# Loading x and the first weight chunk of a two-layer decoder trunk by quarters, with masks and norm vectors loaded later

## The chip, the cores and the metric

The kernel runs on one core of a Trainium2 chip. The metric is device time in microseconds (us) of one execution. Five engines work side by side, each through its own instructions in a fixed order: TensorE (PE in the profile, with its weight loads as PEld), VectorE (DVE), ScalarE (ACT), GpSimd (POOL) and SyncE (SP), which here only issues transfers. Transfers between the chip's main memory (HBM) and the on-chip memories are issued by SP, ACT or POOL and run on 16 DMA engines that all queues share.

## What is computed

The reference runs two post-norm layers on x (256 tokens of 1024 values). Every sub-layer is added to ALPHA times its input and normalized. Only the first feed-forward stage (layer 0, `ffn1`) and the start of the program are touched by the change:

```python
def _post_norm(x, y, g, b):
    z = (ALPHA * x + y).astype(jnp.float32)
    mu = z.mean(-1, keepdims=True)
    var = jnp.square(z - mu).mean(-1, keepdims=True)
    return ((z - mu) * lax.rsqrt(var + LN_EPS) * g + b).astype(x.dtype)

def _swiglu(x, w_in, w_out):
    gate, up = jnp.split(x @ w_in, 2, axis=-1)
    return (jax.nn.silu(gate) * up) @ w_out

for layer in range(DEPTH):
    x = _post_norm(x, FFN_RES_WEIGHT * _swiglu(x, *ffn1[layer]), *ln1[layer])
    mix = ...   # layer 0: short convolution and dilated attention; layer 1: mLSTM and stick-breaking attention
    x = _post_norm(x, mix, *ln2[layer])
    x = _post_norm(x, FFN_RES_WEIGHT * _swiglu(x, *ffn2[layer]), *ln3[layer])
```

## The kernel before

**Weights.** All weight matrices are cut into chunks of 1 MB, numbered in the order of use. Chunk 0 is the gate half of the first 256 columns of the first `w_in`, chunk 1 the up half of the same columns, chunk 2 the next gate half, and so on. The class `Weights` keeps three stages. A chunk is loaded into one of 3 `raw` buffers (`RAW`, line 27) by SP; it is then split in 4 units of a quarter each (`unit`, lines 72 to 91): ACT casts the quarter into a high part `hi` (line 86), and DVE subtracts it from the raw values to make the low part `lo` (line 87). Both lie in one of 5 `hl` buffers. A `raw` buffer can be loaded anew when the last quarter of its chunk has been split, and a later load stands behind an earlier one on SP's queue.

**Matmuls.** x is turned (transposed) on PE, 128 columns at a time, and split in the same way into `xx`, a high and a low part. For each chunk PE makes 16 wide matmuls (`wide`, line 235: `hi` times both parts of x, 128x512) and 16 cross matmuls (`cross`, line 239: `lo` times the high part of x, 128x256), into two PSUM banks out of a pool of four called `mm`. A bank is read out by ACT (line 425) and DVE (line 426, `join`), and only then can a later chunk's matmuls write to it.

**The start.** `start` (line 947) runs under `manual_schedule`: the instructions written in it keep their order among themselves on each engine. Everything else is placed by a scheduler, which may put an instruction of later work between them. PE first makes 9 idle matmuls on a zero tile, turns the first half of x (both token blocks), makes 3 more idle ones and turns the second half. Chunk 0 is then multiplied by quarters, two rows of 128 at a time (`mmB2`, line 252), so that it can begin when the first quarter of the weights and the first half of x are there.

**Transfers at the start.** x comes in four pieces of 256 KB (half a row for each of two token blocks), one block on SP, the other on ACT's queue. Chunks 0 and 1 come in quarters of 256 KB (`load_quarters`, line 48), chunk 2 and all later ones in one transfer. Then stand the masks (`msk`, lines 219 and 221: a pattern of 192 KB and a norm gain of 256 KB), used in the mixers much later, and the gain and bias of the first norm (`gb`, line 225, 512 KB each), used at the end of the stage.

**Scaling.** The residual ALPHA * x is made in place by ACT (line 483), two instructions of 128x1024.

Of the kernel before, what the change touches and what calls it, by code (L numbers as in the profile page):

```python
# [11 lines left out]
F32 = mybir.dt.float32  # L12
# [3 lines left out]
OP = mybir.AluOpType  # L16

P = 128
S = 256
# [3 lines left out]
ALPHA = math.sqrt(2.0)  # L23
# [7 lines left out]
class Weights:  # L31
# [16 lines left out]
    def load_quarters(self):  # L48

        i = self.loaded  # L50
        (ap,), k, c = self.chunks[i]
        self.raw[i] = self.raw_pool.tile([P, k * c], F32, tag="raw", name=f"raw{i}")
        rv = self.raw[i].rearrange("p (k c) -> p k c", k=k)
        for j in range(4):
            self.nc.sync.dma_start(rv[:, 2 * j:2 * j + 2, :], ap[:, 2 * j:2 * j + 2, :])
        self.loaded += 1

    def load(self, upto):
        while self.loaded < min(upto, len(self.chunks)):
# [74 lines left out]
def kernel(ctx: ExitStack, tc: tile.TileContext, a, cmask, out):  # L134
    nc = tc.nc
# [10 lines left out]
    def hp():  # L146
        return tc.high_priority(offset=HP)

    def nm(s):
        uid[0] += 1  # L150
        return f"{s}_{uid[0]}"
# [10 lines left out]
    def GR():  # L162
        return g_pool.tile([P, 1024], F32R, tag="g", name=nm("gr")).rearrange(
            "p (j h t) -> p j h t", j=2, h=2)

    def ACC():
        return ps_acc.tile([P, 512], F32, tag="acc", name=nm("acc"))

    def MM():
        return ps_mm.tile([P, 512], F32, tag="mm", name=nm("mm"))  # L170


    def cols(w, c0):
        return ([a[w][:, c0:c0 + 256].rearrange("(k p) c -> p k c", p=P)], 8, 256)
# [16 lines left out]
    first = cols("l1_mix_w_in", 3080)  # L191
# [5 lines left out]
    W = Weights(nc, raw_pool, w_pool, chunks)  # L197
# [4 lines left out]
    xx = const.tile([P, 8, 2, S], F32R, name="xx")  # L202
    xh, xl = xx[:, :, 0, :], xx[:, :, 1, :]
    X = [const.tile([P, D], F32, name=f"X{t}") for t in range(2)]
    for h in range(2):
        for t in range(2):
            hs = slice(h * 512, (h + 1) * 512)
            (nc.sync, nc.scalar)[t].dma_start(X[t][:, hs], a["x"][0, t * P:(t + 1) * P, hs])
    W.load_quarters()
    W.load_quarters()  # L210
    W.load(RAW)
    ident = const.tile([P, P], F32, name="ident")
    make_identity(nc, ident)
# [2 lines left out]
    Y = const.tile([P, D], F32, name="Y")  # L216
    gb = const.tile([P, 2, D], F32, name="gb")
    msk = const.tile([P, 896], F32, name="msk")
    nc.sync.dma_start(msk[:, 0:384], cmask)
    src = a["l1_mlstm_norm_g"]  # L220
    nc.sync.dma_start(msk[:, 384:896], bass.AP(tensor=src.tensor, offset=src.offset, ap=[[0, P], [1, 512]]))

    def bcast(dst, name, n, eng=None):
        src = a[name]
        (eng or nc.gpsimd).dma_start(dst, bass.AP(tensor=src.tensor, offset=src.offset, ap=[[0, P], [1, n]]))

    def load_gb(pre):
        bcast(gb[:, 0, :], pre + "_g", D, nc.sync)
        bcast(gb[:, 1, :], pre + "_b", D, nc.sync)
# [12 lines left out]
    def mmB1(i, banks, between=None):  # L242

        hi, lo = W.get(i)
        for f, w in ((wide, hi), (cross, lo)):
            if between and f is cross:
                between()
            for j in banks:
                for kt in range(8):
                    f(w, kt, j, banks[j])  # L250

    def mmB2(i, banks):
        hi, lo = W.views(i)
        for kt in range(0, 8, 2):
            for f, w in ((wide, hi), (cross, lo)):
                for j in range(2):
                    for k in (kt, kt + 1):
                        f(w, k, j, banks[j])

    def mmA1(i, t, bank, between=None):  # L260
        hi, _ = W.get(i)
# [37 lines left out]
    def split(hi, lo, src):  # L299
        nc.scalar.copy(hi, src)  # L300
        nc.vector.tensor_tensor(lo, src, hi.bitcast(F32), OP.subtract)  # L301


    def transpose_x(t, halves=(0, 1), scale=True):
        for hf in halves:
            b = MM()
            for j in range(4):
                c = hf * 512 + j * P
                nc.tensor.transpose(b[:, j * P:(j + 1) * P], X[t][:, c:c + P], ident)  # L309
            ks = slice(hf * 4, hf * 4 + 4)  # L310
            ts = slice(t * P, (t + 1) * P)
            with hp():
                split(xh[:, ks, ts], xl[:, ks, ts], b.rearrange("p (k t) -> p k t", k=4))
        if scale:
            nc.scalar.mul(X[t], X[t], ALPHA)
# [91 lines left out]
    def stagger(n, done, mm):  # L407

        ids = W.take(n)
        for t in range(2):  # L410
            for c in range(n):
                if t == 0 and c == n - 1:
                    transpose_x(1)
                b = MM()
                mm(ids[c], t, b)
                if t == 1:
                    W.free(ids[c])
                W.pump()
                done(t, c, b)
# [14 lines left out]
    def swiglu(gate, bank):  # L434

        u = joined(bank)
        nc.vector.scalar_tensor_tensor(u, gate, 0.5, u, OP.mult, OP.mult)  # L437
        return u

    def silu(bank):  # L440
        sg = joined(bank)
        nc.scalar.activation(sg, sg, AF.Silu)  # L442
        return sg

    def ffn(ln, staggered, nxt, last=False):
        ys = []
        todo = []

        def tr(t, gs):
            b = ACC()  # L450
            for p in range(2):
                for j in range(2):
                    nc.tensor.transpose(b[:, (2 * p + j) * P:(2 * p + j + 1) * P],
                                        gs[p][:, j * P:(j + 1) * P], ident)
            ts = slice(t * P, (t + 1) * P)
            for p in range(2):
                split(ys[p][:, :, 0, ts], ys[p][:, :, 1, ts],
                      b[:, p * 256:(p + 1) * 256].rearrange("p (j t) -> p j t", j=2))

        p0 = 0  # L460
        if staggered:
            p0 = 2
            ys = [GR(), GR()]
            gs = {0: [], 1: []}

            half = []

            def done(t, c, bank):
                if c % 2 == 0:
                    half.append(silu(bank))  # L470
                    return
                gs[t].append(swiglu(half.pop(), bank))
                if t == 1 and c == 1:
                    tr(0, gs[0])

            stagger(4, done, mmA1)
            todo.append(lambda: tr(1, gs[1]))
        for p in range(p0, NPAIR):
            if p == 4:
                load_gb(ln)  # L480
                if not staggered:
                    for t in range(2):
                        nc.scalar.mul(X[t], X[t], ALPHA)
            y = GR()
            ys.append(y)
            ig, iu = W.take(2)
            sg = []
            if p == 0:
                banks = [MM(), MM()]
                start(banks)  # L490
                W.pump()
            if p > 0:
                banks = {0: MM(), 1: MM()}
                mmB1(ig, banks)
            W.free(ig)
            for j in range(2):
                sg.append(silu(banks[j]))
                W.pump()
            while todo:
                todo.pop()()  # L500
            banks = {0: MM(), 1: MM()}
            mmB1(iu, banks)
            W.free(iu)
            W.pump()
            for j in range(2):
                g = swiglu(sg[j], banks[j])
                split(y[:, j, 0, :], y[:, j, 1, :], g)
                if j == 0:
                    W.pump()
        out_proj(ys, nxt, last)  # L510
# [436 lines left out]
    def start(banks):  # L947
        def idle(n):
            for _ in range(n):
                nc.tensor.matmul(wb, warm[:, 0:P], warm, start=True, stop=True)  # L950

        wb = MM()
        with tc.manual_schedule():
            idle(9)
            for t in range(2):
                transpose_x(t, (0,), False)
            idle(3)
            W.unit()
            for t in range(2):
                transpose_x(t, (1,), False)  # L960
                W.unit()
            W.unit()
            mmB2(0, banks)

    def f2_1():
        ffn("l1_ln3", True, None, last=True)
# [5 lines left out]
    def f1_1():  # L972
        ffn("l1_ln1", True, m1)

    def f2_0():
        ffn("l0_ln3", True, f1_1)
# [49 lines left out]
```

## Time and profile before

| | us |
|---|---|
| median of 3 runs | 988.82 |
| lowest and highest | 988.48, 989.24 |
| the profiled execution's own time | 989.54 |
| its span, first to last instruction | 987.8 |
| PE busy in the span | 976.6 |
| DVE, ACT, POOL busy | 703.6, 601.3, 24.0 |

A profile row gives a start and a duration in us from the span's first instruction; "idle before" names the idle time of the engine just ahead of the row and what ended it. A row with "x16" joins 16 instructions that follow each other without a gap. The time around the span is 989.54 - 987.8 = 1.74 us. PE is busy in all but some 11 us, so a microsecond counts where PE waits, and those waits lie at the start and at the end.

### The profile page before, as it was taken

To read this page: it belongs to the slowest core of one execution; us is meant where nothing else is said; L and a number is where in the kernel's file an instruction comes from. 1 tells how busy PE (TensorE), PEld (TensorE's weight loads), DVE (VectorE), ACT (ScalarE), POOL (GpSimd) and SP (SyncE) were. 2 spreads that over 40 slices of the span, in tenths; PEclk is the share of its full clock that TensorE was granted. 3 is DMA by queue.
4 is the path that set the end of the run, shared out by engine and by line. 5 is a ranking of instruction groups with operands and counts; after the bars stand their busy time and mean duration, and the time that the engine had idled before them with its cause. 6 is when DMAs were issued, how large, how long until landed. Compare 5 with 4: busy or idle time off the path is not lost.

```text
span 987.8 us, 14559 instructions
## 1 busy us (share of the span) xinstructions
PE 976.6 (99%) x5408; PEld 843.3 (85%) x5408; DVE 703.6 (71%) x1466; ACT 601.3 (61%) x1307; POOL 24.0 (2%) x62
## 2 busy tenths in 40 slices
PE   9999999999999999999999999999999999999997
PEld 7888888888878888888888888888888888888886
DVE  4987764678958877754687777547997788777534
ACT  6875654559847756553566665436887676565520
POOL 2000000010000000000000000001000100000000
PEclk9999999999999999999999999999999999999999
DMA  9875556474426756465475554646734267565611
GB/s 322 290 244 186 196 188 208 134 257 144 155 85 214 251 177 204 178 208 177 151 256 188 190 194 173 212 128 214 233 133 146 86 213 256 179 206 171 212 45 42
DMA packets 137495, 183.89 MB, mean 186 GB/s; under 512 B 4304, under 2 KB 121680, under 8 KB 137424
## 3 DMA queue, kind: packets, MB, share of 16 engines
q1 hardware_dynamic: 136720, 182.17, 55.4%
q8 instruction: 42, 0.69, 0.3%
q10 hardware_dynamic: 576, 0.79, 0.2%
q0 software_dynamic: 128, 0.01, 0.1%
q14 instruction: 29, 0.24, 0.1%
HBM read 181.90 MB, written 1.05 MB: 185 GB/s over the span
## 4 chain that ended last, share of the span: by engine, by line
PE 93%; DMA 2%; DVE 2%; ACT 2%; issue 0%; POOL 0%; DVEq 0%; POOLq 0%; ACTq 0%
PE mm L235 33%; PE mm L239 17%; PE acc L293 9%; PE acc L297 9%; PE acc L295 9%; PE mm L265 7%; PE mm L270 4%; DMA raw<-in_l_ffn_w_in_dram 2%; DVE hl L87 1%; PE acc L606 1%; PE mm L309 1%; PE mm L552 1%; ACT hl L86 1%; PE acc L546 0%; PE acc L547 0%; DMA X<-in_x_dram 0%
## 5 line engine op out<-in xcount | busy, mean ns | idle before, releaser
L87 DVE TENSOR_TENSOR hl<-raw,hl 128x512 fp32r<-128x512 f32 (+1 forms) x664 | 427.1, 687 | 89.1 <-ACT hl L86 82.7
L86 ACT CAST hl<-raw 128x512 fp32r<-128x512 f32 (+1 forms) x664 | 379.7, 621 | 108.8 <-PE acc L297 43.2
L235 PE MATMUL mm<-xx,hl 128*128 128x512 f32 x1472 | 357.4, 392 | 2.1 <-DVE t L426 1.1
L235 PEld LDWEIGHTS mm<-xx,hl 128*128 128x128 f32 x1472 | 269.0, 188 | 55.5 <-DVE t L426 1.7
L239 PEld LDWEIGHTS mm<-xx,hl 128*128 128x128 f32 x1472 | 189.8, 191 | 7.2
L239 PE MATMUL mm<-xx,hl 128*128 128x256 f32 x1472 | 195.4, 284 | 0.0
L425 ACT COPY t<-mm 128x256 f32<-128x256 f32 x182 | 66.7, 369 | 139.1 <-PE mm L239 127.3
L426 DVE TENSOR_TENSOR t<-mm,t 128x256 f32<-128x256 f32 x182 | 76.9, 424 | 97.2 <-ACT t L425 94.7
L293 PE MATMUL acc<-hl,gr 128*128 128x512 f32 (+1 forms) x416 | 128.7, 387 | 0.0
L295 PE MATMUL acc<-hl,gr 128*128 128x512 f32 (+1 forms) x416 | 127.5, 384 | 0.0
L297 PE MATMUL acc<-hl,gr 128*128 128x512 f32 (+1 forms) x416 | 127.1, 384 | 0.0
L297 PEld LDWEIGHTS acc<-hl,gr 128*128 128x128 f32 x416 | 77.1, 188 | 15.3 <-DVE gr L301 0.4
L295 PEld LDWEIGHTS acc<-hl,gr 128*128 128x128 f32 x416 | 77.2, 188 | 15.1
L293 PEld LDWEIGHTS acc<-hl,gr 128*128 128x128 f32 x416 | 76.0, 188 | 14.6 <-issue 0.6
L265 PE MATMUL mm<-hl,xx 128*128 128x512 f32 x336 | 85.1, 395 | 0.1
L265 PEld LDWEIGHTS mm<-hl,xx 128*128 128x128 f32 x336 | 60.5, 189 | 11.2 <-DVE t L426 0.3
L442 ACT ACTIVATE t<-t 128x256 f32<-128x256 f32 x88 | 36.7, 419 | 22.6 <-DVE t L426 22.5
L270 PEld LDWEIGHTS mm<-hl,xx 128*128 128x128 f32 x336 | 45.6, 190 | 3.1
L270 PE MATMUL mm<-hl,xx 128*128 128x256 f32 x336 | 47.1, 283 | 0.0
L328 ACT ACTIVATE t<-X,st 128x512 bf16<-128x512 f32 x22 | 15.7, 716 | 50.7 <-DVE st L324 50.7
L322 DVE SCALAR_TENSOR_TENSOR X<-acc,X 128x512 f32<-128x512 f32 x22 | 14.3, 690 | 42.3 <-PE acc L297 42.3
L437 DVE SCALAR_TENSOR_TENSOR t<-t,t 128x256 f32<-128x256 f32 x88 | 37.4, 425 | 2.6
(166 smaller groups left out, 565.3 us busy)
## 6 DMA issues: line engine op xcount, KB each, us to landing
raw<-in_l_ffn_w_in_dram SPq DMA_DIRECT2D x86, 1024.0 KB, 5.0
raw<-in_l_ffn_w_out_dram SPq DMA_DIRECT2D x44, 1024.0 KB, 4.9
raw<-in_l_mix_w_in_dram SPq DMA_DIRECT2D x26, 1024.0 KB, 5.2
raw<-in_l_mix_w_out_dram SPq DMA_DIRECT2D x8, 1024.0 KB, 4.9
gb<-in_l_ln_g_dram SPq DMA_DIRECT2D x6, 512.0 KB, 5.5
gb<-in_l_ln_b_dram SPq DMA_DIRECT2D x6, 512.0 KB, 5.1
raw<-in_l_ffn_w_in_dram SPq DMA_DIRECT2D x8, 256.0 KB, 7.3
X<-in_x_dram ACTq DMA_DIRECT2D x2, 256.0 KB, 4.3
```

The costliest lines, as they stand in the source:

```text
L86: self.nc.scalar.copy(hi[at], r[at])
L87: self.nc.vector.tensor_tensor(lo[at], r[at], hi[at].bitcast(F32), OP.subtract)
L235: nc.tensor.matmul(bank, hi[:, kt, j * P:(j + 1) * P], xx[:, kt].rearrange("p h t -> p (h t)"), start=kt == 0, stop=False)
L239: nc.tensor.matmul(bank[:, S:2 * S], lo[:, kt, j * P:(j + 1) * P], xh[:, kt, :], start=False, stop=kt == 7)
L265: nc.tensor.matmul(bank, xh[:, kt, ts], hl[:, kt].rearrange("p h c -> p (h c)"), start=kt == 0, stop=False)
L270: nc.tensor.matmul(bank[:, 256:512], xl[:, kt, ts], hi[:, kt, :], start=False, stop=kt == 7)
L293: nc.tensor.matmul(accs[c][:, 0:w], yh, hi[:, k, c:c + w], start=st, stop=False)
L295: nc.tensor.matmul(accs[c][:, 0:w], yh, lo[:, k, c:c + w], start=False, stop=False)
L297: nc.tensor.matmul(accs[c][:, 0:w], yl, hi[:, k, c:c + w], start=False, stop=sp)
L425: nc.scalar.copy(dst, bank[:, 256:512])
L426: nc.vector.tensor_tensor(dst, bank[:, 0:256], dst, OP.add)
L437: nc.vector.scalar_tensor_tensor(u, gate, 0.5, u, OP.mult, OP.mult)
```

## The change

It has four parts. (1) x comes in eight quarters of 128 KB (256 columns of a token block), and SP issues a quarter of x and a quarter of chunk 0 in turn; ACT issues the other block's four quarters. (2) `start` turns x by quarters into banks of the pool `acc`, splits each with `keep`, and puts the turning of the third and fourth quarter behind the matmuls of the first and second. (3) The masks, and the gain and bias of the first norm, are loaded at the fifth column pair (p == 4): GpSimd writes two values of `ys[3]` (the result of the fourth pair) into `msk` and `gb`, and the transfers that overwrite these must wait for that. (4) The two scalings of x move from ACT to GpSimd.

```diff
     def load_quarters(self):
         i = self.loaded
+        self.loaded += 1
         (ap,), k, c = self.chunks[i]
         self.raw[i] = self.raw_pool.tile([P, k * c], F32, tag="raw", name=f"raw{i}")
         rv = self.raw[i].rearrange("p (k c) -> p k c", k=k)
         for j in range(4):
             self.nc.sync.dma_start(rv[:, 2 * j:2 * j + 2, :], ap[:, 2 * j:2 * j + 2, :])
-        self.loaded += 1
+            yield
...
-    for h in range(2):
+    first = W.load_quarters()
+    for q in range(4):
+        qs = slice(q * 256, (q + 1) * 256)
         for t in range(2):
-            hs = slice(h * 512, (h + 1) * 512)
-            (nc.sync, nc.scalar)[t].dma_start(X[t][:, hs], a["x"][0, t * P:(t + 1) * P, hs])
-    W.load_quarters()
-    W.load_quarters()
+            (nc.sync, nc.scalar)[t].dma_start(X[t][:, qs], a["x"][0, t * P:(t + 1) * P, qs])
+        next(first)
+    for _ in W.load_quarters():
+        pass
     W.load(RAW)
...
-    nc.sync.dma_start(msk[:, 0:384], cmask)
-    src = a["l1_mlstm_norm_g"]
-    nc.sync.dma_start(msk[:, 384:896], bass.AP(tensor=src.tensor, offset=src.offset, ap=[[0, P], [1, 512]]))
+    def load_msk():
+        nc.sync.dma_start(msk[:, 0:384], cmask)
+        src = a["l1_mlstm_norm_g"]
+        nc.sync.dma_start(msk[:, 384:896], bass.AP(tensor=src.tensor, offset=src.offset, ap=[[0, P], [1, 512]]))
...
-    def mmB2(i, banks):
+    def mmB2(i, banks, kt):
         hi, lo = W.views(i)
-        for kt in range(0, 8, 2):
-            for f, w in ((wide, hi), (cross, lo)):
-                for j in range(2):
-                    for k in (kt, kt + 1):
-                        f(w, k, j, banks[j])
+        for f, w in ((wide, hi), (cross, lo)):
+            for j in range(2):
+                for k in (kt, kt + 1):
+                    f(w, k, j, banks[j])
...
             if p == 4:
+                if not staggered:
+                    late = ys[3].bitcast(F32)
+                    nc.gpsimd.tensor_copy(msk[:, 0:385:384], late[:, 0, 0, 0:2])
+                    nc.gpsimd.tensor_copy(gb[:, :, 0:1], late[:, :, 0, 0:1])
+                    load_msk()
+                    for t in range(2):
+                        nc.gpsimd.tensor_scalar(X[t], X[t], ALPHA, None, op0=OP.mult)
                 load_gb(ln)
-                if not staggered:
-                    for t in range(2):
-                        nc.scalar.mul(X[t], X[t], ALPHA)
...
+        def turned(q):
+            b = ACC()
+            for t in range(2):
+                for k in range(2):
+                    c = (2 * q + k) * P
+                    nc.tensor.transpose(b[:, k * S + t * P:k * S + (t + 1) * P], X[t][:, c:c + P], ident)
+            return b
+
+        def keep(q, b):
+            ks = slice(2 * q, 2 * q + 2)
+            split(xh[:, ks, :], xl[:, ks, :], b.rearrange("p (k t) -> p k t", k=2))
+
         wb = MM()
         with tc.manual_schedule():
             idle(9)
-            for t in range(2):
-                transpose_x(t, (0,), False)
+            b0 = turned(0)
+            W.unit()
+            keep(0, b0)
             idle(3)
+            b1 = turned(1)
+            keep(1, b1)
             W.unit()
-            for t in range(2):
-                transpose_x(t, (1,), False)
-                W.unit()
-            W.unit()
-            mmB2(0, banks)
+            for q in range(4):
+                mmB2(0, banks, 2 * q)
+                if q < 2:
+                    b = turned(q + 2)
+                    keep(q + 2, b)
+                    W.unit()
```

The diff does not tell where the scheduler puts the instructions, so the order in the two built programs is shown at three places.

The first place is ACT's queue from the first cast on. In the kernel before, `hl_144` and `raw_88` are chunk 0, `hl_202` and `raw_93` chunk 1, `hl_221` chunk 2, and `mm_127` to `mm_156` the banks with turned x. Before:

```order
L300 CAST xx<-mm_127 128x4x128
L300 CAST xx<-mm_134 128x4x128
L86 CAST hl_144<-raw_88 128x2x256
L300 CAST xx<-mm_147 128x4x128
L86 CAST hl_144<-raw_88 128x2x256
L300 CAST xx<-mm_156 128x4x128
L86 CAST hl_144<-raw_88 128x2x256 x2
L86 CAST hl_202<-raw_93 128x2x256 x4
L86 CAST hl_221<-raw_98 128x2x256 x3
L425 COPY t_207<-mm_113 128x256
```

After the change `hl_134` and `raw_86` are chunk 0, `hl_204` and `raw_97` chunk 1, `hl_223` and `raw_102` chunk 2, and `acc_129`, `acc_142`, `acc_159`, `acc_176` the four turned quarters of x:

```order
L87 CAST hl_134<-raw_86 128x2x256
L87 CAST hl_204<-raw_97 128x2x256 x2
L305 CAST xx<-acc_129 128x2x256
L87 CAST hl_204<-raw_97 128x2x256 x2
L305 CAST xx<-acc_142 128x2x256
L87 CAST hl_134<-raw_86 128x2x256
L305 CAST xx<-acc_159 128x2x256
L87 CAST hl_134<-raw_86 128x2x256
L87 CAST hl_223<-raw_102 128x2x256 x2
```

Casts of chunks 1 and 2 now stand between those of x and chunk 0: two quarters of chunk 1 ahead of the first quarter of x. On DVE the subtractions stand in the same order, one for each of these casts.

The second place follows on ACT's queue right behind the rows above; `hl_274` and `raw_185` are chunk 3, and `mm_115` is the first of chunk 0's two banks:

```order
L305 CAST xx<-acc_176 128x2x256
L87 CAST hl_134<-raw_86 128x2x256
L87 CAST hl_223<-raw_102 128x2x256 x2
L87 CAST hl_274<-raw_185 128x2x256 x2
L430 COPY t_209<-mm_115 128x256
L430 COPY t_219<-mm_116 128x256
```

The read of chunk 0's banks stands behind two casts of chunk 3 here; before, it stood behind three of chunk 2 (the last two rows of the first fence). On DVE one subtraction of chunk 3 stands ahead of its part of that read.

The third place is SP's queue. Before, the masks and the first norm's vectors stood between chunk 2 (`raw_98`) and chunk 3 (`raw_167`):

```order
L67 DMA raw_98<-in_l_ffn_w_in_dram 128x8x256
L219 DMA msk<-pattern_mask_dram 128x384
L221 DMA msk<-in_l_mlstm_norm_g_dram 128x512
L225 DMA gb<-in_l_ln_g_dram 128x1024
L225 DMA gb<-in_l_ln_b_dram 128x1024
L67 DMA raw_167<-in_l_ffn_w_in_dram 128x8x256
```

After the change they stand between chunk 14 (`raw_780`) and chunk 15 (`raw_829`), and SP waits there for GpSimd's two small copies:

```order
L68 DMA raw_780<-in_l_ffn_w_in_dram 128x8x256
L224 DMA msk<-pattern_mask_dram 128x384
L226 DMA msk<-in_l_mlstm_norm_g_dram 128x512
L230 DMA gb<-in_l_ln_g_dram 128x1024
L230 DMA gb<-in_l_ln_b_dram 128x1024
L68 DMA raw_829<-in_l_ffn_w_in_dram 128x8x256
```

Four transfers of 1.44 MB (1472 KB) together moved behind twelve chunks; nothing else on SP's queue changed its place except x and chunk 0, which now alternate.

## Rows read from the trace of the kernel before

**Rows 1.** The page: busy time; share of the chain; three groups with mean ns; 1 MB loads.

```profile
PE 976.6 (99%) x5408; PEld 843.3 (85%) x5408; DVE 703.6 (71%) x1466; ACT 601.3 (61%) x1307; POOL 24.0 (2%) x62
...
PE 93%; DMA 2%; DVE 2%; ACT 2%; issue 0%; POOL 0%; DVEq 0%; POOLq 0%; ACTq 0%
...
L87 DVE TENSOR_TENSOR hl<-raw,hl 128x512 fp32r<-128x512 f32 (+1 forms) x664 | 427.1, 687 | 89.1 <-ACT hl L86 82.7
L86 ACT CAST hl<-raw 128x512 fp32r<-128x512 f32 (+1 forms) x664 | 379.7, 621 | 108.8 <-PE acc L297 43.2
...
raw<-in_l_ffn_w_in_dram SPq DMA_DIRECT2D x86, 1024.0 KB, 5.0
```

**Rows 2.** Chain of waits, first 60 us: start, duration, what.

```profile
4.59 7.21 DMA raw<-in_l_ffn_w_in_dram
...
11.82 0.64 ACT hl L86
...
12.48 0.50 DVE hl L87
12.98 11.10 DMA raw<-in_l_ffn_w_in_dram
...
24.76 1.29 DVE hl L87 x2
26.05 0.35 DVE t L426
...
26.44 3.94 PE mm L235 x16
```

**Rows 3.** Timeline, first 32 us: start, duration, engine, line, operation, [idle before].

```profile
1.26 3.54 PE L950 MATMUL mm<-warm 128*128 128x512 bf16 x9 [1.26 <-DVE warm L201]
...
5.95 0.54 POOL L861 TENSOR_SCALAR_AFFINE_SELECT mc<-mc 128x128 f32<-128x128 f32 x2
6.15 1.04 PE L309 MATMUL mm<-ident,X 128*128 128x128 f32 x8
...
8.02 0.58 ACT L300 CAST xx<-mm 128x512 fp32r<-128x512 f32 x1
...
8.17 1.20 PE L235 MATMUL mm<-xx,hl 128*128 128x512 f32 x4 [0.98 <-ACT hl L86]
...
8.76 0.68 DVE L301 TENSOR_TENSOR xx<-mm,xx 128x512 fp32r<-128x512 f32 x1
...
14.01 3.82 PE L235 MATMUL mm<-xx,hl 128*128 128x512 f32 x16
...
18.17 0.64 ACT L425 COPY t<-mm 128x256 f32<-128x256 f32 x2
...
19.22 1.07 ACT L483 ACTIVATE X<-X 128x1024 f32<-128x1024 f32 x1
...
19.57 3.82 PE L235 MATMUL mm<-xx,hl 128*128 128x512 f32 x16
...
25.97 0.42 DVE L426 TENSOR_TENSOR t<-mm,t 128x256 f32<-128x256 f32 x1
```

**Rows 4.** Timeline of SP at 5 us.

```profile
5.00 0.56 SPq L55 DMA_DIRECT2D raw<-in_l_ffn_w_in_dram  x1
```

**Rows 5.** Transfers issued at 5 us: KB each, us to landing.

```profile
raw<-in_l_ffn_w_in_dram SPq DMA_DIRECT2D x1, 256.0 KB, 7.5
```

**Rows 6.** Stretches: length, busy PE, PEld, DVE, ACT, POOL; PEclk, DMA share, GB/s.

```profile
2.00:11.00 9.00, 8.02 (x43) 5.47 (x41) 3.78 (x6) 4.75 (x8) 4.36 (x13) 1.00 0.97 285
980.00:988.00 8.00, 0.64 (x6) 0.44 (x4) 4.17 (x10) 0.00 (x0) 0.99 (x1) 0.74 0.19 66
```

**Rows 7.** Timeline of SP at 61 us.

```profile
61.17 0.37 SPq L67 DMA_DIRECT2D raw<-in_l_ffn_w_in_dram  x1
```

**Rows 8.** Timeline of PE at 93 us.

```profile
93.90 3.82 PE L235 MATMUL mm<-xx,hl 128*128 128x512 f32 x16
```

## The prediction, made before the change was run

> **What bounds the kernel now.** I read the page first: PE is busy 976.6 of 987.8 us and holds 93% of the chain of waits [rows 1]. So time is won or lost where PE waits, and I went on to the chain at the start [rows 2]. It shows two waits. PE's first real matmul stands at 8.17 us, after the 9 idle matmuls and the turning of x, when the first cast of weights is done [rows 3]. The second is before chunk 3: its load is issued at 12.98, when DVE has finished splitting chunk 0 and so has freed the `raw` buffer; it lands 11.10 us later, at 24.08; then come casts, two subtractions and one read of a bank by DVE (26.05 to 26.40), and only then PE starts chunk 3, at 26.44 [rows 2]. The timeline gives PE's own pace between these: chunk 0 from 8.17 to 14.01 (1.46 us a quarter), chunk 1 from 14.01 to 19.57, so 5.56 us for a chunk [rows 3]. Chunk 2 would end at 19.57 + 5.56 = 25.1, so about 1.3 us of PE time are lost before 26.44. After that PE runs through, and what shifts the start of chunk 3 shifts the end.
>
> So the most that the change can win is small: the start before 8.17, and 1.3 us. What it can lose depends on the orders of ACT and DVE, shown at the first two places in the section on the change. ACT and DVE take their instructions strictly in the order of their queues, and in the changed program two quarters of chunk 1 stand ahead of the first quarter of x. PE's first real matmul needs that quarter of x, high and low part.
>
> **The start: when the first matmul can come.** Let L be the time at which chunk 1's second quarter lands. Before, it was issued at 5.00 and landed 7.5 us later [rows 4, 5], so L = 12.50. Behind x and chunk 0 it is the same 2.62 MB from the start in both programs (x 1.05, chunk 0 1.05, half of chunk 1 0.52), and the masks stood behind it before as well, so I take 12.5. The bounds: the DMA engines moved 285 GB/s between 2 and 11 us [rows 6], and 2.62 MB at that mean rate are in at 11.2; on the other side SP now has two more issues ahead of it (ten instead of eight, since x makes four pieces on each queue), at 0.56 us each [rows 4], so 13.6.
>
> From L on: ACT casts that quarter (0.62), DVE subtracts it (0.69), then comes the low part of x's first quarter (0.68; its cast on ACT, 0.58, lies beside the subtraction) [rows 1, 3]. First matmul: 12.5 + 0.62 + 0.69 + 0.68 = 14.5, against 8.17. PE has nothing to do from the turning of x's second quarter (7.2 at the latest, as before [rows 3]) until then, some 7 us.
>
> **From there to the end of chunk 0.** On DVE twelve instructions of 0.69 stand from that subtraction to the last one of chunk 0 (three of chunk 1, two of chunk 2, three of chunk 0, four of x): chunk 1, x, chunk 1, chunk 1, x, chunk 0, x, chunk 0, chunk 2, chunk 2, x, chunk 0. Unhindered they end at 12.5 + 0.62 + 12 x 0.69 = 21.4. But the seventh, x's third quarter, needs PE to have turned it, and that now stands behind the first quarter of chunk 0's matmuls. Here the clock counts. The first nine idle matmuls of 128x512 took 3.54 us, 0.39 each, while sixteen of the same width later took 3.82, 0.24 each [rows 3]: PE begins at the lower of its levels. At the end of the kernel, where PE worked 0.64 of the last 8 us, the mean granted clock of the stretch was 0.74, so it had fallen to the lower level in it [rows 6]. The 7 us of waiting at the start are of the same kind, so I take it that the clock has fallen when PE resumes at 14.5. Then the first quarter takes 2 x 1.46 and the turning of four blocks 1.04 instead of 0.52 (eight took 1.04 [rows 3]): 14.5 + 2.92 + 1.04 = 18.5; cast and subtraction of x, 0.58 + 0.68, end at 19.7, where the unhindered chain had 12.5 + 0.62 + 7 x 0.69 = 17.9. So the chain is 1.8 late, and chunk 0 is split at 23.2. If the clock stays up, it is 21.4; that is the other end.
>
> **Chunk 3's load, and the wait that takes the old one's place.** Chunk 3 can't be loaded before that split, as before at 12.98 [rows 2]. So its issue moves from 12.98 to 23.2. With nothing else under way by then a 1 MB load lands in 5.0 us [rows 1]: 28.2, against 24.08. That the masks and vectors (1472 KB, at 285 GB/s 5.2 us of transfers) are gone from the start therefore wins nothing: their place is taken by waiting for a buffer. On ACT the read of chunk 0's first bank stands behind two casts of chunk 3 (second place): 28.2 + 2 x 0.62 + 0.32 for the read (two took 0.64) + 0.42 for DVE's part [rows 3] = 30.2. Chunk 2's matmuls need that bank (before, the same row of DVE released chunk 3 [rows 2]). PE itself could be through chunk 1 about 5.56 after chunk 0's split, at 28.8. So the bank decides: chunk 2 starts at 30.2, chunk 3 at 30.2 + 5.56 = 35.8, where its data has long been split. Against 26.44 that is **+9.3 us**.
>
> **The other parts, costed at nothing.** ACT loses two instructions of 1.07 us at 19 to 23 us [rows 3]; in that stretch of the new program ACT waits for chunk 3's load, so nothing is won. GpSimd takes them: its nearest row is 0.54 us for two of 128x128 [rows 3], so 128x1024 would be up to 2.2 us each, 4.3 together, against ACT's 1.07 each; it has nothing else to do until the first norm, far behind. The two small copies are of the same kind and shorter. SP then waits for GpSimd's copies ahead of chunk 15's load (third place). That wait ends when the fourth pair is done, which is chunk 7: 26.44 + 5 x 5.6 + some 3 = 57.5 on the old scale, while chunk 15's load was issued at 61.17 anyway [rows 7], and PE needs it at 93.90 [rows 8]. So SP is not kept; were the wait longer than that, it has some 28 us of cover, and the four transfers' 5.2 us fit as well. The two further issues of x on ACT lie before its first cast. What remains is the same work on the same engines, and I count +0 for it.
>
> The sum is made in the span of the profiled execution, 987.8, and lies wholly in it, so it carries over to the median, which is 0.72 below that execution's 989.54: 988.82 + 9.3 = **998.1 us**.
>
> **The rivals.**
>
> *Same mechanism, clock stays up or data is earlier.* The chain ends at 21.4 instead of 23.2: +7.5, 996.3. With L at its lower bound 11.2 as well: +6.2, 995.0. For it speaks that the clock's fall is seen in one row at the end only; against it, that PE waits as long here. With L at 13.6 and the clock down it is +10.4, 999.2.
>
> *GpSimd gets in DVE's way.* Scaling x now runs beside DVE's last subtractions for chunk 0, from about 21 us. If they were stretched to twice their length while GpSimd works on the first block (2.2 us), the split of chunk 0 would come some 1.1 to 2.2 later: 999.2 to 1000.3. In the only row of the kind, two GpSimd instructions at 5.95 to 6.49 beside the subtraction of x, that subtraction is no longer than others; but it reads one of its inputs from PSUM. The Trainium skill says in GPSIMD Engine Reference, section Key points, that GpSimd shares its SBUF interfaces with VectorE and that the two contend when VectorE's instruction has two SBUF inputs, as the subtractions of weights have; by that rule this rival would hold, and no row here shows it.
>
> *Faster: the change does what its words say.* If the casts of x and chunk 0 did not stand behind chunk 1's, PE could start when x's first quarter is turned after the idle matmuls: 4.8 + 0.52 + 0.58 + 0.68 = 6.6, 1.6 sooner, of which chunk 1's landing would leave perhaps a third; and chunk 3's wait of 1.3 would go, since 1472 KB fewer stand ahead of it. Together -1.9: 986.9. It decides only if L is 5.3 or less, the time at which x's first quarter is turned; for a transfer that was issued at 5.00 this is out of reach. What is left for it is that I misread which engine waits for what.
>
> **How the numbers follow.** Forecast (clock down, +8.5 to +10.5) 0.55; clock up or data earlier (+6 to +8.5) 0.27; GpSimd in the way 0.08; faster 0.07; the rest, within 0.2% (2 us, about what a measurement can tell here), 0.03. The predicted time is that of the likeliest, 998.1. The range takes in the second and third case: from 994.5, just under the lower bound of L with the clock up, to 1000.5. Faster 0.07, same 0.03, slower 0.90.
>
> **What would show it.** Right: in the changed profile PE's first L240 row stands at 14 to 15 us with some 7 us of idle time before it; ACT's first cast of x (L305) stands behind two casts of weights at about 13; chunk 3's load is issued at 21 to 23.5, with the DMA engines idle from about 17; matmuls at 14.5 take twice the time of those at 20; PE waits once more, at about 29, for DVE's L431. Wrong: a first L240 row before 9 us; a load of chunk 3 before 17 us; a chunk 3 that starts before 33 us; or PE waits in the middle of the stage, with SP waiting for GpSimd's copies.

## The result, and the profile after the change

The kernel became slower: 996.74 us in the median (996.57 to 997.20) against 988.82 (988.48 to 989.24), a ratio of 1.0081, with a 95% interval from 1.0070 to 1.0092. The profiled execution of after took 996.74 us with a span of 995.0; against the profiled execution of before (989.54, span 987.8) that is +7.2, and by the medians +7.9.

The page of after: busy times, the shares of the chain, and PE's largest group with the idle time before it.

```profile
PE 978.5 (98%) x5408; PEld 844.9 (85%) x5408; DVE 705.5 (71%) x1466; ACT 598.2 (60%) x1305; POOL 31.5 (3%) x66
...
PE 94%; ACT 2%; DVE 2%; DMA 1%; issue 0%; POOL 0%; ACTq 0%; DVEq 0%; SPq 0%; POOLq 0%
...
L240 PE MATMUL mm<-xx,hl 128*128 128x512 f32 x1472 | 358.3, 393 | 7.2 <-DVE xx L306 6.4
```

PE is 1.9 us longer busy than in [rows 1], and has some 5 us more of idle time. The list of PE's waits in after (who waits for whom: us in total, times, the longest) says where:

```profile
PE mm L240 <- DVE xx L306: 6.4, 1, 6.4
PE mm L960 <- DVE warm L202: 1.3, 1, 1.3
PE mm L240 <- ACT hl L87: 0.8, 1, 0.8
```

The 1.3 is there in [rows 3] as well. New are one wait of 6.4 for x's low part, and one of 0.8. The chain of waits of after (start, duration, what) shows how the first comes about:

```profile
7.53 4.48 DMA raw<-in_l_ffn_w_in_dram
...
12.03 0.63 ACT hl L87
...
12.68 0.52 DVE hl L88
...
13.29 0.69 DVE xx L306
...
14.03 2.07 PE mm L240 x4
```

The transfer that lands at 12.01 is the second quarter of chunk 1, and PE's first real matmul needs nothing of it: it only stands ahead of x's first quarter on ACT and DVE. In [rows 2] the first transfer of the chain landed at 11.80, and PE had been at work since 8.17 by then. The timeline of after, 9 to 35 us (start, duration, engine, line, operation, idle before):

```profile
11.38 1.27 ACT L87 CAST hl<-raw 128x512 fp32r<-128x512 f32 x2 [5.46 <-DMA raw<-in_l_ffn_w_in_dram]
...
12.55 0.58 ACT L305 CAST xx<-acc 128x512 fp32r<-128x512 f32 x1
...
13.89 1.28 DVE L88 TENSOR_TENSOR hl<-raw,hl 128x512 fp32r<-128x512 f32 x2
...
14.03 2.07 PE L240 MATMUL mm<-xx,hl 128*128 128x512 f32 x4 [6.41 <-DVE xx L306]
...
15.20 0.37 SPq L68 DMA_DIRECT2D raw<-in_l_ffn_w_in_dram  x1
...
17.26 1.17 PE L240 MATMUL mm<-xx,hl 128*128 128x512 f32 x4
...
18.16 0.69 DVE L306 TENSOR_TENSOR xx<-acc,xx 128x512 fp32r<-128x512 f32 x1 [1.78 <-ACT xx L305]
...
19.23 2.86 POOL L492 TENSOR_SCALAR X<-X 128x1024 f32<-128x1024 f32 x1 [12.18 <-PE acc L968]
...
19.36 1.52 DVE L88 TENSOR_TENSOR hl<-raw,hl 128x512 fp32r<-128x512 f32 x1
...
21.41 0.68 DVE L306 TENSOR_TENSOR xx<-acc,xx 128x512 fp32r<-128x512 f32 x1
...
22.07 3.26 POOL L492 TENSOR_SCALAR X<-X 128x1024 f32<-128x1024 f32 x1
...
22.24 1.17 PE L240 MATMUL mm<-xx,hl 128*128 128x512 f32 x4 [0.80 <-ACT hl L87]
...
22.61 1.52 DVE L88 TENSOR_TENSOR hl<-raw,hl 128x512 fp32r<-128x512 f32 x1
...
22.72 0.37 SPq L68 DMA_DIRECT2D raw<-in_l_ffn_w_in_dram  x1
...
28.62 3.82 PE L240 MATMUL mm<-xx,hl 128*128 128x512 f32 x16
...
34.19 3.82 PE L240 MATMUL mm<-xx,hl 128*128 128x512 f32 x16
```

Read from top to bottom: ACT waits 5.46 us for chunk 1, x follows, PE begins at 14.03 at the slow pace (2.07 for four wide matmuls; the next four, at 17.26, take 1.17). Chunk 3's load is issued at 15.20, right behind the end of chunk 1's split on DVE (13.89 + 1.28 = 15.17). The wait of 0.80 at 22.24 is put down to ACT, which had long been done; what ends at 22.09 is DVE's work on x's last quarter, at 21.41; ahead of it stands the subtraction that took 1.52 beside GpSimd. Chunk 2 starts at 28.62 and chunk 3 at 34.19, with no wait between them.

The stretches of after (length; busy PE, PEld, DVE, ACT, POOL; PEclk, DMA share, GB/s) show the clock:

```profile
14.00:18.00 4.00, 3.97 (x15) 3.49 (x16) 2.37 (x4) 1.64 (x4) 0.00 (x0) 0.62 0.71 230
18.00:22.00 4.00, 3.45 (x21) 2.71 (x19) 3.84 (x5) 4.00 (x9) 2.77 (x1) 1.00 0.42 148
```

The sum of the difference, in profiles: the first matmul comes 14.03 - 8.17 = 5.86 later; from there to chunk 2 it takes 14.59 us instead of 11.40 [rows 3], 3.19 more; from chunk 2 to chunk 3 5.57 instead of 6.87 [rows 2, 3], 1.30 less; and from chunk 3 to the matmul of [rows 8], which is at 100.99 in after, 66.80 instead of 67.46, 0.66 less. Together +7.09, of the 7.2 by the spans: nothing of size is lost or won behind that matmul, at about 100 us.

### The profile page after: what moved, and what is told of

It reads as the page before. It is cut to its first block, busy times and chain, and to the rows that moved or that the text cites. A ratio compares the mean times of both kernels' runs of the same rounds, so it can differ in the third digit from the quotient of the medians.

```text
span 995.0 us, 14570 instructions
## 1 busy us (share of the span) xinstructions
PE 978.5 (98%) x5408; PEld 844.9 (85%) x5408; DVE 705.5 (71%) x1466; ACT 598.2 (60%) x1305; POOL 31.5 (3%) x66
## 4 chain that ended last, share of the span: by engine, by line
PE 94%; ACT 2%; DVE 2%; DMA 1%; issue 0%; POOL 0%; ACTq 0%; DVEq 0%; SPq 0%; POOLq 0%
PE mm L240 33%; PE mm L244 17%; PE acc L298 9%; PE acc L302 9%; PE acc L300 9%; PE mm L270 7%; PE mm L275 4%; ACT hl L87 1%; PE acc L616 1%; DVE hl L88 1%; PE mm L314 1%; PE mm L562 1%; DMA X<-in_x_dram 1%; PE acc L556 0%; DMA raw<-in_l_ffn_w_in_dram 0%; PE acc L557 0%
```

## Experiments

The theory: the loss is the order of ACT's and DVE's queues at the start. `start` names the splits of chunk 0 and of x, but not those of chunk 1, and the scheduler put two of these ahead of x's first quarter. The rivals: the new form of the start itself makes it (eight pieces of x, turning between the matmuls), or GpSimd's scaling does, beside DVE.

**The order as written.** After the change, with the four splits of chunk 1 written into the manual stretch, behind all that chunk 0 needs.

```diff
             for q in range(4):
                 mmB2(0, banks, 2 * q)
                 if q < 2:
                     b = turned(q + 2)
                     keep(q + 2, b)
                     W.unit()
+            for _ in range(4):
+                W.unit()
```

> The changed kernel, with the four splits of chunk 1 written into the hand-ordered start behind chunk 0's matmuls, so that nothing stands between the casts of x and chunk 0. Theory A (the order: x waits on ACT and DVE behind two casts of chunk 1): the first real matmul comes at 7.5 to 8 us instead of 14.03, chunk 2 starts at about 20.5 instead of 28.6, and the time is 987 to 988.5 us, 8 to 9.5 below the changed kernel. Rival B (the pieces: quarters of x in turn with quarters of chunk 0 come in later than the larger pieces did): the first matmul stays late, above 11 us, and the time stays above 993. Rival C (GpSimd's scaling or the held-back loads cost the time): they are still in it, so it stays at 995 to 997.

Measured: 988.00 (987.66 to 989.05) against 988.85 of before on the same chip, ratio 0.9990 (0.9982 to 0.9999). The timeline of PE:

```profile
7.56 1.17 PE L240 MATMUL mm<-xx,hl 128*128 128x512 f32 x4
...
9.04 0.60 PE L968 MATMUL acc<-ident,X 128*128 128x128 f32 x4
9.40 1.18 PE L240 MATMUL mm<-xx,hl 128*128 128x512 f32 x4
...
14.44 3.81 PE L240 MATMUL mm<-xx,hl 128*128 128x512 f32 x16
...
20.00 3.82 PE L240 MATMUL mm<-xx,hl 128*128 128x512 f32 x16
...
25.56 3.82 PE L240 MATMUL mm<-xx,hl 128*128 128x512 f32 x16
```

The quarters of x, the turning between matmuls, GpSimd's scaling and the late masks are all still in it, and the whole loss is gone: the order decides. It also tells what the start by quarters is worth by itself. The first matmul comes 0.61 sooner than at 8.17, but chunk 0 and 1 take 12.44 us instead of 11.40, since the turning that stood ahead now stands between the quarters (0.36 for each of the two, 9.04 to 9.40), and some 0.3 us go ahead of the last quarter. Chunk 2 starts at 20.00, later than in before (19.57), and chunk 3 at 25.56, sooner than 26.44. Against before this kernel is faster by under a thousandth, and no version of the study is clearly faster than it.

**The order alone.** Before, with two splits of chunk 1 put ahead of x's first split and nothing else changed (a buffer is counted as free when all four quarters are split, whichever came first).

```diff
         wb = MM()
+        W.plan[0:8] = [W.plan[k] for k in (4, 5, 0, 1, 2, 3, 6, 7)]
         with tc.manual_schedule():
             idle(9)
+            W.unit()
+            W.unit()
             for t in range(2):
                 transpose_x(t, (0,), False)
```

> The kernel before, with only one thing of the change: the first two splits of chunk 1 stand ahead of x's first split on ACT and DVE. Pieces, masks and scaling are as before. Theory A: the first real matmul comes when chunk 1's second quarter has landed (12.5) and about 2.6 us of casts and subtractions are done, at 15 us; PE's clock has fallen by then, chunk 2 starts at about 28, and the time is 994 to 996.5 us. Rival B (the pieces make the loss): 988.8, first matmul at about 8.

Measured: 995.74 (995.61 to 996.48), ratio 1.0067 (1.0053 to 1.0081). Timeline, ACT and PE:

```profile
11.48 1.31 ACT L87 CAST hl<-raw 128x512 fp32r<-128x512 f32 x2 [8.46 <-DMA raw<-in_l_ffn_w_in_dram]
12.69 1.07 ACT L303 CAST xx<-mm 128x512 fp32r<-128x512 f32 x2
...
14.17 1.12 PE L312 MATMUL mm<-ident,X 128*128 128x128 f32 x4 [6.96 <-DVE xx L304]
14.94 2.06 PE L238 MATMUL mm<-xx,hl 128*128 128x512 f32 x4
```

The same picture as after, in a kernel without any other part of the change: the order is not only needed for the loss, it is enough for 6.9 of the 7.9 us.

**The whole order by hand, and PE kept at work.** For experiments on what hangs on the order, the order of after was written out (12 splits permuted as below, in the places where the scheduler had put them), and then 24 idle matmuls were added where PE waits (`idle(24)` in place of the `idle(0)` below).

```diff
+        W.plan[0:12] = [W.plan[k] for k in (0, 4, 5, 6, 7, 1, 2, 8, 9, 3, 10, 11)]
...
             b1 = turned(1)
+            idle(0)
+            W.unit()
+            W.unit()
             keep(1, b1)
```

> The changed kernel's own order of the first stage, written out by hand; nothing else. It is the pair to e4_clock_kept_up. All theories: first matmul at about 14, as in the changed kernel, and 996 to 997 us.

> The changed kernel's own order of the first stage, written out by hand so that the scheduler can't move it, plus 24 idle matmuls behind the turning of x's second quarter, so that PE works through its wait of 6.4 us. It differs from e4z_same_order in these idle matmuls alone. Theory (the clock had fallen when PE resumed): chunk 0's first four wide matmuls take 1.0 to 1.2 us instead of 2.07, the clock's row for 14 to 18 us is 1.00 instead of 0.62, chunk 0 is done some 1.0 to 1.8 us sooner, and the time is 995 to 995.8 us. Rival (DVE's chain of twelve instructions sets the end of chunk 0 whatever PE's clock is): 996.5, as e4z.

Measured: 996.59 (996.41 to 997.17), ratio 1.0081 (1.0067 to 1.0094), without idle matmuls, as after; 995.17 (994.84 to 995.66), ratio 1.0065 (1.0053 to 1.0078), with 24. The timelines of PE and the stretch from 14 to 18 us (columns as above), first without:

```profile
13.52 2.08 PE L243 MATMUL mm<-xx,hl 128*128 128x512 f32 x4 [5.84 <-DVE xx L309]
...
28.19 2.00 PE L243 MATMUL mm<-xx,hl 128*128 128x512 f32 x8
```

```profile
14.00:18.00 4.00, 4.00 (x15) 3.42 (x15) 2.00 (x5) 1.70 (x5) 0.00 (x0) 0.50 0.78 264
```

With the idle matmuls:

```profile
7.93 5.34 PE L963 MATMUL mm<-warm 128*128 128x512 bf16 x24
13.99 1.21 PE L243 MATMUL mm<-xx,hl 128*128 128x512 f32 x4 [0.71 <-DVE xx L309]
...
20.85 1.16 PE L243 MATMUL mm<-xx,hl 128*128 128x512 f32 x4 [0.79 <-ACT hl L88]
...
27.21 3.14 PE L243 MATMUL mm<-xx,hl 128*128 128x512 f32 x13
```

```profile
14.00:18.00 4.00, 4.00 (x25) 3.62 (x26) 3.56 (x7) 2.99 (x7) 0.16 (x1) 1.00 0.74 253
```

The lower level (0.50 of full speed, 1.2 GHz) is gone, the first four matmuls take 1.21 instead of 2.08, and from the first matmul to chunk 2 it takes 13.22 us instead of 14.67. The two kernels differ in one more thing that follows from this: without idle matmuls the clock stays at 0.50 until about 19 us (in after until about 17), and GpSimd's scaling, which starts only just ahead of x's last quarter there (19.86), delays nothing that PE waits for; with them it does, and PE waits 0.79 at 20.85, as it waits 0.80 in after. So after itself is the better partner: its first matmul stands at 14.03 against 13.99, it has the same wait, and its chunk 2 starts at 28.62 against 27.21. The clock's fall is shown, and costs 1.4 us of the loss; the wait for chunk 1 itself stays.

**Chunk 1 in one transfer.** The written-out order (without idle matmuls), with chunk 1 loaded as one piece of 1 MB.

```diff
-    for _ in W.load_quarters():
-        pass
     W.load(RAW)
```

> As e4z_same_order, but chunk 1 is loaded in one transfer of 1 MB instead of four quarters, so the casts that stand ahead of x can begin only when all of it has landed, at about 13.1 instead of 12.0. Theory A (PE's start hangs on chunk 1's landing): the first matmul comes at landing + 0.62 + 0.62 + 0.69 + 0.68 = 2.6 us after it, 15.5 to 16 instead of 14.0, and the time is 997.8 to 998.6. Rival (it hangs on x's or chunk 0's quarters): first matmul at 14.0, 996.5 us.

Measured: 998.53 (998.38 to 1000.35), ratio 1.0105 (1.0090 to 1.0121). Timeline:

```profile
13.12 1.14 ACT L88 CAST hl<-raw 128x512 fp32r<-128x512 f32 x2 [7.30 <-DMA raw<-in_l_ffn_w_in_dram]
...
15.71 2.08 PE L241 MATMUL mm<-xx,hl 128*128 128x512 f32 x4 [7.82 <-DVE xx L307]
```

With nothing of x or chunk 0 touched, PE's start moves by 2.2 us and the time by 1.9: it hangs on the landing of chunk 1.

**Scaling back on ACT.** After, with the two scalings of x on ACT.

```diff
-                    for t in range(2):
-                        nc.gpsimd.tensor_scalar(X[t], X[t], ALPHA, None, op0=OP.mult)
                 load_gb(ln)
+                if not staggered:
+                    for t in range(2):
+                        nc.scalar.mul(X[t], X[t], ALPHA)
```

> The changed kernel, with the two scalings of x back on ACT; the order of the start's casts is the same. In the changed kernel two of DVE's subtractions took 1.52 us instead of 0.68 while GpSimd scaled x, the first of them ahead of x's last quarter, and PE stood 0.80 us there. Theory A with this as a side cost: those two subtractions take 0.68 again, PE's wait of 0.80 goes, 995.9 us (-0.8). Rival C (the scaling on GpSimd is the main cost): about 989. Rival: the long subtractions have another cause and stay, 996.7.

Measured: 996.22 (995.28 to 996.68), ratio 1.0069 (1.0057 to 1.0082). Timeline, DVE and PE:

```profile
18.10 0.69 DVE L306 TENSOR_TENSOR xx<-acc,xx 128x512 fp32r<-128x512 f32 x1 [1.42 <-ACT xx L305]
18.71 1.88 DVE L88 TENSOR_TENSOR hl<-raw,hl 128x512 fp32r<-128x512 f32 x3
20.51 0.68 DVE L306 TENSOR_TENSOR xx<-acc,xx 128x512 fp32r<-128x512 f32 x1
...
27.68 2.68 PE L240 MATMUL mm<-xx,hl 128*128 128x512 f32 x11
```

Three subtractions take 1.88 together, where one of after's took 1.52 alone, x's last quarter stands at 20.51 instead of 21.41, and PE's 0.80 is gone. From the first matmul (13.66) to chunk 2 it takes 14.02 instead of 14.59, 0.57 less. But the clock came back later here (granted clock 0.53 from 17.0 to 17.5 us, where after has 0.95), so that the way to x's third quarter took 0.31 more (13.66 to 18.10, against 14.03 to 18.16). From that quarter to chunk 2, the stretch that GpSimd touches, it is 9.58 instead of 10.46. So GpSimd costs some 0.9 of the 7.9 in after's profile: a side cost, of the size expected. The two medians differ by 0.5 only and their runs overlap (after's lowest is 996.57, this kernel's highest 996.68), so it rests on the profile more than on the times. With it the 3.19 more between the first matmul and chunk 2 can be roughly made up: 1.4 for the clock, 0.9 for GpSimd, and the 1.04 that the start by quarters takes longer even in the right order (12.44 against 11.40).

**The written order with scaling on ACT.** The first experiment, with `nc.scalar.mul` for the two halves behind chunk 1's splits in the manual stretch, in place of GpSimd's instructions.

> As e1_order_as_written, and the two scalings of x on ACT again, placed behind the casts of chunk 1, where ACT waited 1.7 us for chunk 2. DVE's subtractions are no longer stretched by GpSimd (0.68 all through). In e1 that stretching fell where little waited for it (0.28 us of PE idle time), so by the theory it is 987.6 to 988.0, 0 to 0.4 us below e1. Rival (the stretch cost e1 as much as it cost the changed kernel, 0.8): 987.2.

Measured: 988.07 (987.77 to 988.96), ratio 0.9993 (0.9984 to 1.0002), not to be told from the first experiment's 988.00. With the order right, DVE has room for GpSimd's disturbance.

**Only the masks held back.** Before, with the two copies on GpSimd and the later loads of masks and vectors, and nothing else.

```diff
             if p == 4:
+                if not staggered:
+                    late = ys[3].bitcast(F32)
+                    nc.gpsimd.tensor_copy(msk[:, 0:385:384], late[:, 0, 0, 0:2])
+                    nc.gpsimd.tensor_copy(gb[:, :, 0:1], late[:, :, 0, 0:1])
+                    load_msk()
                 load_gb(ln)
```

> The kernel before, with only the masks and the first norm's vectors held back to the fifth pair by the same two small GpSimd copies; x, the start and the scaling on ACT are as before. Theory: chunk 3's load, issued at about 13, lands at about 18 instead of 24.1, PE's wait before chunk 3 (1.1 to 1.3 us) goes, and the small losses of chunks 3 to 7 (0.66 us by comparing the two profiles) go too: 986.9 to 987.7 us. Rival (the held-back loads cost something in the middle of the stage, since SP waits there for GpSimd): 989 or more. Rival (nothing depends on them): 988.8.

Measured: 988.58 (988.05 to 989.76), ratio 0.9996 (0.9988 to 1.0005): the expected gain did not come. So the kernel before was profiled twice more, unchanged.

> The kernel before, unchanged, profiled a second time, to see how much its start differs between executions: the first profile was of an execution of 989.54 us, 0.7 above the median, and e3_masks_late_only measured 0.3 us below the kernel before where 1.1 to 1.9 was expected. If the wait before chunk 3 differs between executions (reason A: 1.1 us in that profile was on the high side), chunk 3 starts well before 26.44 here, at 25.4 to 26.0, in an execution near 988.8. If it is always there (reason B: e3 gives its gain back later), chunk 3 starts at 26.3 to 26.5 again.

> A third look at the kernel before, with the same question as b2_before_again and the same two answers.

Measured: 989.48 and 988.05. Chunk 3's start on PE's timeline, first in these two executions of before, then with the masks held back:

```profile
25.78 1.43 PE L235 MATMUL mm<-xx,hl 128*128 128x512 f32 x5 [0.31 <-DVE t L426]
```

```profile
25.21 3.93 PE L235 MATMUL mm<-xx,hl 128*128 128x512 f32 x16
```

```profile
25.35 3.94 PE L237 MATMUL mm<-xx,hl 128*128 128x512 f32 x16
```

In [rows 2] this row stands at 26.44, behind a wait. So the wait ahead of chunk 3 is 1.1 us in one execution, 0.3 in another and nothing in a third: holding the masks back can win it only where it is there, and with it gone chunk 3 starts where the third execution has it anyway. What varies is the landing of chunk 3's load: issued at 12.98, 13.18 and 12.33 in the three executions of before, it took 11.1, 10.2 and 10.5 us and landed at 24.1, 23.4 and 22.8. With the masks held back it was issued at 12.41 and took 6.7, so it landed at 19.1, five microseconds sooner than in the first; but ACT casts it at 23.03 only, right behind its second scaling of x, and PE is busy with chunk 2 until 25.35 in any case.

## Why the prediction was right, and where it was off

The sign, the place and the mechanism held, and 996.74 lies in the range of 994.5 to 1000.5; the forecast of 998.1 was 1.4 too high. By its own steps:

- **Landing of chunk 1's second quarter (12.5), first matmul (14.5).** It landed at 12.01, and the three links behind it took 2.0 as summed: 14.03. Half a microsecond too much, inside the bounds.
- **The clock falls.** Held, shown by the 0.62 in 14 to 18 us, the 2.07 against 1.17, and the idle matmuls that hold it at 1.00. But it was back sooner than I took it: the second quarter's wide matmuls at 17.26 were at full speed, and x's third quarter was split at 18.85, not 19.7 (0.47 of these 0.85 us are the earlier first matmul). That PE starts the program at the lower level was read from the pace of the first idle matmuls, 0.39 each; the granted clock of [rows 6] reads 1.00 for 2 to 11 us and doesn't show it. The pace bears it out: the 24 idle matmuls of the same form took 0.22 each.
- **Chunk 0 split at 23.2.** It was 22.69 (the load of 22.72 follows it). Close, with some luck, since two errors cancel: the 0.85 just named, and 0.84 for a subtraction that GpSimd stretched, which stood in a rival and not in the forecast. The half microsecond that is left comes from the length of a link: subtractions that follow each other start 0.60 apart (three in 1.88 without GpSimd), and the sum had 0.69.
- **Chunk 3's load can't be issued before that split: the step that failed.** It was issued at 15.20, not 23.2, as the text itself named for a sign against it ("a load of chunk 3 before 17 us"). I carried the rule of [rows 2] over, where chunk 0's split frees the buffer for chunk 3. In the new order chunk 1 is split before chunk 0, so that its buffer is free first: by the times, chunk 3 took that one (split done at 15.17, load at 15.20), and chunk 4 took chunk 0's (22.69 and 22.72). The order of splits had been in the rows shown ahead of the prediction; I used it for x and not for the buffers. With the data there by about 20, no bank waits behind late casts: ACT and DVE read the banks by 26.0, not 30.2, and PE starts chunk 2 when it is through with chunk 1, at 28.62, without the wait that was expected at about 29. The prediction had 28.8 for just this case and dropped it. Chunk 3 so started at 34.19 instead of 35.8: the 1.6 by which the forecast was off at that place.
- **The wait of 1.3 that goes.** It went, and another 0.66 of small losses behind it, as measured against the profiled execution of before. But two more executions show that this part varies by itself. I counted the sum in a profile that was 0.7 slower than the median and added it to the median, as if every execution had lost as much ahead of chunk 3. In the three executions of before chunk 7 starts at 49.37, 48.87 and 47.98, and they took 989.54, 989.48 and 988.05: of the 1.49 between the first and the third, 1.39 is lost by then, in waits that after doesn't have; the second loses its lead of 0.50 over the first further on. That is how +7.2 by the profiles goes with +7.9 by the medians. It is luck, too: by the profiles +9.3 was 2.1 too high, and the slow profile it was counted in brings that down to the 1.4 by the medians.
- **GpSimd costed at nothing, up to 2.2 us each.** Too low on both counts: 2.86 and 3.26 us, and DVE was hindered. The rival said that subtractions would be up to twice their length; one for each GpSimd instruction was (1.52 against 0.68), the others not. The first delays x's last quarter and makes PE's 0.80, and the price is some 0.9 by the profiles and 0.5 by the medians. The Trainium skill's GPSIMD Engine Reference, section Key points, says that GpSimd and VectorE contend where VectorE's instruction has two SBUF inputs; this trace agrees in part: both stretched subtractions have two, and x's at 21.41, with one input in PSUM, took 0.68 beside GpSimd, but so did other subtractions of weights.
- **SP's wait for GpSimd's copies.** Costed at nothing, and so it was. After's mask loads on SP, and chunk 15's behind them:

```profile
64.25 0.34 SPq L224 DMA_DIRECT2D msk<-pattern_mask_dram  x1
...
66.68 0.38 SPq L68 DMA_DIRECT2D raw<-in_l_ffn_w_in_dram  x1
```

  Chunk 15's load goes out 5.5 later than in [rows 7], and PE needs it at 100.99, 7.1 later than in [rows 8].

Of the rivals, the faster one falls with 14.03 for the first matmul, and the first experiment shows what became of its size: the first matmul did come 0.61 sooner there (7.56), but the turning between the quarters took that back before chunk 2 (20.00 against 19.57), and the wait it counted on is not always there. Of its -1.9, -0.85 was measured. The rival with the clock up, at +7.5, was nearest in number and wrong in cause: the kernel with 24 idle matmuls, where the clock does stay up, takes 6.3 more than before.

## What to carry to other kernels

A change to the start of a kernel is also a change to what the scheduler does with all that is not written down there: read the built order of each in-order engine, and ask of every instruction that stands ahead of the first useful one what it waits for. Use the same order for the buffers too: which one comes free first decides when the next load goes out. And before a wait of a microsecond is counted as a gain, look whether it is there in a second and third execution.

## What the runs showed of the hardware

- A GpSimd multiplication of 128x1024 float values in place took 2.86 and 3.26 us in after (2.86 to 3.29 in the five kernels of the study that scale on GpSimd), where ACT took 1.07 [rows 3].
- In after, the next VectorE instruction to begin once a GpSimd multiplication had begun (19.23 and 22.07) was a subtraction with both inputs in SBUF, and it took 1.52 us instead of 0.68 (19.36 and 22.61). The following ones were at 0.68 again, though GpSimd was still at work. In the first experiment the next one behind GpSimd's start at 11.36 was a subtraction of x, with one input in PSUM (12.13): it took 0.69, and the three subtractions of weights behind it, all begun while GpSimd was at work, 0.68 each. Behind GpSimd's second start there (14.22) a subtraction of weights was next, and took 1.52. The written-out order without idle matmuls and the kernel with chunk 1 in one transfer show the same. So what was stretched here was only the next instruction, and only where both its inputs were in SBUF.
- After 6.4 us without work PE came back at the lower level of its clock, four wide matmuls in 2.07 us, and at 17.26 four took 1.17 again. With 24 idle matmuls in the gap, and 0.71 us left empty, it did not fall.
